# Down-projections of two feed-forward networks by Strassen's seven products, and the order of the second mixer's tiles

## The chip, the cores and the metric

One core of one Trainium2 chip runs the whole program. The metric is the device time of one execution in microseconds. Three runs of the kernel before took 2653.42, 2655.38 and 2654.62 us; the median is 2654.62 us. The profiled execution, from which all rows come, is a run of its own.

## The reference

Two transformer-like blocks run one after the other on a sequence of 1024 positions of width 1024, in float32. Each has a mixer and a feed-forward network (FFN). Cut to what the change touches, with x of shape 1024 x 1024:

```python
# first block: D_FF = 2816, second block: 4096
a, b = split(dwconv3(rms_norm(x) @ w_up), 2)     # w_up: 1024 x 5632
x = x + gate * rms_norm((gelu(a) * b) @ w_down)  # w_down: 2816 x 1024
...                                              # second mixer: four branches, gates
h = rms_norm(x) @ w_up_2                         # 1024 x 4096
x = x + rms_norm(square(relu(h)) @ w_down_2)     # w_down_2: 4096 x 1024
```

The two products by `w_down` and `w_down_2` are the down-projections. Their inner dimension is 22 and 32 tiles of 128 hidden units.

## The kernel before, in words

A float32 matrix is kept as a pair of narrower ones, a high part (fp32r, made by a cast on ScalarE) and a low part (what is left, made by a subtraction on VectorE): `split`, L345 to L347. One product is then three matmuls, high by high, high by low and low by high. All large matmuls are of one size: a stationary block of 128 x 128 and a moving one of 128 x 512.

The up-projections and the gates of the second mixer already use Strassen's scheme (`strassen`, L205 to L258). It takes a pair of weight blocks as a 2 x 2 matrix of blocks and the activations as another, and makes seven products (84 matmuls) where eight would do. The sums of activation quarters that the products need are made once per stage by `act_sums` (L318 and the splits behind it), the sums of weights by `_pair` (L144).

The down-projections don't. `ffn` (L615 to L640) computes hidden units and stores each tile of 128 units, 512 KB, to DRAM through ScalarE's DMA queue (L619, tensors `hd`). `Down` (L565 to L612) then takes the units in groups of k-tiles, 2, 2, 2, 4, 4, 4, 4 in the first FFN and 2, 2 and seven times 4 in the second. For a k-tile, `prep` loads the weight tile and the hidden tile (512 KB each, issued by SyncE, L583) and splits both. For a group, `rows` (L485 to L500) goes through the eight row tiles of the output, and for each through the k-tiles of the group with six matmuls each; `rows_sum` adds the two PSUM halves to the output tile in SBUF (copies by ScalarE in the first group, L507, VectorE additions afterwards, L509). `prep` of the next group stands between the row tiles.

In the second mixer, before the gates, a short convolution (`sc_y`, L1411 to L1418) and `act_sums` are written one after the other, in the order three steps of the convolution, a half of the sums, one step, the other half, the rest (L1780 to L1787). The results of the branches go to DRAM (`br`, L1733) and come back (`st`) for the branch projections.

Each engine executes its instructions in order. That order is set when the kernel is built, by a scheduler that works from the program as it is written and from the buffers of the tile pools. A tile pool with n buffers makes the writer of tile i wait until all readers of tile i - n have finished.

Of the kernel before, what the change touches and what calls it, by code (L numbers as in the profile page):

```python
# [55 lines left out]
def drive(*streams):  # L56
# [3 lines left out]
    while live:  # L60
# [50 lines left out]
class Weights:  # L111
# [72 lines left out]
    def next(self, n=1, room=None, slow=False):  # L184
# [4 lines left out]
        if self.begun < len(self.units):  # L189
# [123 lines left out]
def act_sums(k, act, place, tmp):  # L313
# [8 lines left out]
    for j in range(2):  # L322
# [239 lines left out]
class Down:  # L562
# [25 lines left out]
    def first(self):  # L588
        for _ in range(self.sizes[0]):
            self.prep(0)  # L590

    def run(self, pool, bnd):
        k = self.k
        Y = [pool.tile([P, T], F32, name=f"y{m}") for m in range(8)]
        n = len(self.sizes)
        for G in range(n):
# [7 lines left out]
            for tt in range(8):  # L604
                ps = (row_halves if last or tt % 2 == 0 else row_pair)(k)
                rows(k, parts, lhs, tt, ps)
                rows_sum(k, ps, Y[tt], G == 0)
                if last:
                    bnd.row(Y, tt)
                elif tt % 2 == 1 and len(self.got) < self.sizes[G + 1]:  # L610
                    self.prep(G + 1)


def ffn(k, w, act, n, head, tail, sizes, bnd):
# [3 lines left out]
    hd = [k.dp.tile([P, T], F32, name=f"hd{n}_{i}") for i in range(n)]  # L618
    out = lambda i, t: k.nc.scalar.dma_start(out=hd[i], in_=t)  # L619
    with ExitStack() as whole:  # L620
# [3 lines left out]
        dn = Down(k, w, hd, sizes, place)  # L624
        with ExitStack() as c:
# [15 lines left out]


def ffn1(k, w, act, bnd):
# [27 lines left out]
    def head(spare, sums, out):  # L671
        pg, pv = halves(k, w, act)
        next(sums)
# [4 lines left out]
        next(sums)  # L678
# [1446 lines left out]
```

## Time and profile before

| | |
|---|---|
| median of three runs | 2654.62 us |
| profiled execution | 2655.48 us |
| its span, first to last instruction | 2653.7 us |
| TensorE matmuls busy | 2565.7 us, 11972 matmuls |
| VectorE busy | 1793.3 us |
| ScalarE busy | 1080.3 us |
| DMA | 267.07 MB |

Outside the span lie 1.8 us. Busy shares are means over stages with different limits, so the rows below are taken by stage. Between 560 and 900 us the first FFN's up-projection runs, from 928 to about 1160 its down-projection, up to about 1465 and beyond the second mixer, from 1468 its gates, from 2298 the second down-projection. In a timeline a bracket behind an instruction holds the idle time of its engine just before it and what ended it.

### The profile page before, as it was taken

To read this page: it belongs to the slowest core of one execution; us is meant where nothing else is said; L and a number is where in the kernel's file an instruction comes from. 1 tells how busy PE (TensorE), PEld (TensorE's weight loads), DVE (VectorE), ACT (ScalarE), POOL (GpSimd) and SP (SyncE) were. 2 spreads that over 40 slices of the span, in tenths; PEclk is the share of its full clock that TensorE was granted. 3 is DMA by queue.
4 is the path that set the end of the run, shared out by engine and by line. 5 is a ranking of instruction groups with operands and counts; after the bars stand their busy time and mean duration, and the time that the engine had idled before them with its cause. 6 is when DMAs were issued, how large, how long until landed. Compare 5 with 4: busy or idle time off the path is not lost.

```text
span 2653.7 us, 30737 instructions
## 1 busy us (share of the span) xinstructions
PE 2565.7 (97%) x11972; PEld 2090.8 (79%) x11972; DVE 1793.3 (68%) x2882; ACT 1080.3 (41%) x1604; POOL 0.2 (0%) x4
## 2 busy tenths in 40 slices
PE   5999999899999999999999899999999999999998
PEld 4886777778888788878877688888878888888886
DVE  8778757888888863385779765665667545454435
ACT  6444746544444431174343433233365444521211
POOL 0000000000000000000000000000000000000000
PEclk9999999899999999999999999999999999999999
DMA  7315424122222352131012222222342333642312
GB/s 256 97 51 171 136 64 151 54 87 80 84 75 96 130 187 80 48 132 48 32 40 73 78 80 77 98 80 73 103 150 88 103 119 103 204 136 97 107 53 103
DMA packets 85653, 267.07 MB, mean 101 GB/s; under 512 B 12545, under 2 KB 22145, under 8 KB 85506
## 3 DMA queue, kind: packets, MB, share of 16 engines
q1 hardware_dynamic: 76002, 230.49, 26.4%
q10 hardware_dynamic: 9504, 34.61, 3.3%
q8 instruction: 94, 1.54, 0.2%
q14 instruction: 53, 0.43, 0.1%
HBM read 210.53 MB, written 54.53 MB: 100 GB/s over the span
## 4 chain that ended last, share of the span: by engine, by line
PE 83%; DVE 10%; ACT 3%; DMA 2%; issue 1%; SPq 0%; ACTq 0%; DVEq 0%
PE ps_p L233 23%; PE ps_q L233 12%; PE ps_row L496 5%; PE ps_row L498 5%; PE ps_row L500 5%; PE ps_rows L496 4%; PE ps_rows L498 4%; PE ps_rows L500 4%; PE ps_z L217 3%; PE ps_z L213 3%; PE ps_z L215 3%; PE ps_bo L217 1%; PE ps_bo L215 1%; PE ps_bo L213 1%; PE ps_o L1177 1%
## 5 line engine op out<-in xcount | busy, mean ns | idle before, releaser
L346 ACT CAST whi<-wraw 128x1024 fp32r<-128x1024 f32 x232 | 243.2, 1051 | 516.1 <-DVE wraw L144 156.8
L347 DVE TENSOR_TENSOR wlo<-wraw,whi 128x1024 fp32r<-128x1024 f32 x232 | 283.0, 1222 | 174.9 <-ACT whi L346 174.6
L233 PE MATMUL ps_p<-s,whi 128*128 128x512 f32 x792 | 247.0, 393 | 0.2 <-DVE s L347 0.2
L509 DVE TENSOR_TENSOR y<-y,ps_row 128x512 f32<-128x512 f32 x160 | 103.3, 682 | 136.9 <-PE ps_row L500 136.9
L233 PEld LDWEIGHTS ps_p<-s,whi 128*128 128x128 f32 x792 | 148.9, 188 | 33.6 <-DVE s L347 0.6
L233 PE MATMUL ps_p<-s,wlo 128*128 128x512 f32 x396 | 155.3, 392 | 0.0
L509 DVE TENSOR_TENSOR y<-y,ps_rows 128x512 f32<-128x512 f32 x112 | 71.8, 682 | 109.9 <-PE ps_rows L500 109.9
L233 PE MATMUL ps_q<-s,whi 128*128 128x512 f32 x408 | 125.9, 389 | 0.3 <-ACT y L245 0.3
L375 ACT ACTIVATE junk<-y 128x1024 bf16<-128x1024 f32 x56 | 59.1, 1056 | 154.8 <-DVE y L481 69.8
L144 DVE TENSOR_TENSOR wraw<-wraw,wraw 128x512 f32<-128x512 f32 x150 | 103.7, 691 | 11.5 <-DMA wraw<-in_W 7.1
L240 DVE TENSOR_TENSOR sg<-sg,ps_p 128x512 f32<-128x512 f32 x79 | 54.1, 685 | 69.2 <-PE ps_p L233 63.6
L240 DVE TENSOR_TENSOR y<-y,ps_p 128x512 f32<-128x512 f32 x85 | 58.1, 684 | 49.3 <-PE ps_p L233 48.6
L240 DVE TENSOR_TENSOR y<-y,ps_q 128x512 f32<-128x512 f32 x83 | 56.8, 684 | 48.9 <-PE ps_q L233 48.7
L346 ACT CAST s<-s 128x1024 fp32r<-128x1024 f32 x30 | 31.6, 1053 | 143.1 <-PE ps_rows L498 124.2
L233 PEld LDWEIGHTS ps_q<-s,whi 128*128 128x128 f32 x408 | 76.5, 188 | 16.6 <-ACT y L245 0.7
L233 PEld LDWEIGHTS ps_p<-s,wlo 128*128 128x128 f32 x396 | 74.5, 188 | 16.6
L346 ACT CAST dnh<-s 128x1024 fp32r<-128x1024 f32 x24 | 25.2, 1049 | 134.9 <-PE ps_rows L498 120.5
L233 PE MATMUL ps_q<-s,wlo 128*128 128x512 f32 x204 | 79.4, 389 | 0.0
L496 PE MATMUL ps_row<-whi,s 128*128 128x512 f32 x240 | 75.3, 393 | 3.2 <-ACT y L507 1.8
L500 PE MATMUL ps_row<-whi,s 128*128 128x512 f32 x240 | 75.1, 393 | 0.0
L498 PE MATMUL ps_row<-wlo,s 128*128 128x512 f32 x240 | 74.7, 391 | 0.0
L498 PE MATMUL ps_rows<-dnl,dnh 128*128 128x512 f32 x192 | 59.1, 389 | 0.0
(734 smaller groups left out, 6762.9 us busy)
## 6 DMA issues: line engine op xcount, KB each, us to landing
wraw<-in_W SPq DMA_DIRECT2D x216, 512.0 KB, 3.8
s<-hd SPq DMA_DIRECT2D x54, 512.0 KB, 4.7
scr<-in_wa SPq DMA_DIRECT2D x32, 512.0 KB, 4.3
hd<-y ACTq DMA_DIRECT2D x28, 512.0 KB, 4.7
xr<-y SPq DMA_DIRECT2D x24, 512.0 KB, 2.8
hd<-cg ACTq DMA_DIRECT2D x22, 512.0 KB, 2.6
wa<-in_wa SPq DMA_DIRECT2D x16, 512.0 KB, 4.8
xl<-xr SPq DMA_DIRECT2D x16, 512.0 KB, 4.8
```

Of the source, the lines that this page charges most:

```text
L144: less = lambda o, x, y: self.k.nc.vector.tensor_tensor(out=o, in0=x, in1=y, op=ALU.subtract)
L213: nc.tensor.matmul(ps(h), lhsT=wh, rhs=xh[:, cut(h)], start=a, stop=False)
L215: nc.tensor.matmul(ps(h), lhsT=wh, rhs=xl[:, cut(h)], start=False, stop=False)
L217: nc.tensor.matmul(ps(h), lhsT=wl, rhs=xh[:, cut(h)], start=False, stop=z)
L233: mm = lambda x, y, start=False, stop=False: nc.tensor.matmul(ps, lhsT=x, rhs=y, start=start, stop=stop, skip_group_check=True)
L240: add = lambda o, x, y: V.tensor_tensor(out=o, in0=x, in1=y, op=ALU.add)
L346: k.nc.scalar.copy(hi, x)
L347: k.nc.vector.tensor_tensor(out=lo, in0=x, in1=rr(hi), op=ALU.subtract)
L496: nc.tensor.matmul(ps[c], lhsT=xh, rhs=wh[:, S2H[c]], start=a, stop=False)
L498: nc.tensor.matmul(ps[c], lhsT=xh, rhs=wl[:, S2H[c]], start=False, stop=False)
L500: nc.tensor.matmul(ps[c], lhsT=xl, rhs=wh[:, S2H[c]], start=False, stop=z)
L509: k.V.tensor_tensor(out=o, in0=o, in1=ps[c], op=ALU.add)
```

## The change

The down-projections take most of their hidden tiles four at a time. Such a batch is a 2 x 2 matrix of blocks on the side of the hidden units (two k-tiles by 512 positions each) and on the side of the weights (two k-tiles by 512 outputs). It goes through seven products, in the order p1, p6, p2, p7, p5, p4, p3. A product of one batch is a step: 24 matmuls, into four PSUM banks. The batches of a group go through a product one after the other, and its banks are summed over them; then the banks are added to the output tiles or to a partial sum `u`. `DOWN1` has one group of four batches, then plain groups of 2 and 4 k-tiles; `DOWN2` has groups of four and three batches, then a plain group of 4. The plain groups keep the old code.

`load` issues the DMAs of a step three steps ahead: a hidden quarter or a weight quarter is 512 KB, in runs of 2 KB. `prep` makes the factors of a step two steps ahead: sums (L645), then splits (L360, L361). The split hidden factor has three buffers (`s4`/`s5`, `s6`/`s7`, `s8`/`s9` by step number modulo 3), the split weight factor three, the raw hidden tiles four in rotation.

In the second mixer `act_sums` hands back control four times per half, short convolution and sums are interleaved by `drive` with costs, and the temporaries of the sums are in a pool of their own.

```diff
-    def run(self, pool, bnd):
-        k = self.k
-        Y = [pool.tile([P, T], F32, name=f"y{m}") for m in range(8)]
+    ORDER = ("p1", "p6", "p2", "p7", "p5", "p4", "p3")
+    AHEAD = 2
...
+        self.steps = [(g, p, b) for g, nb in enumerate(groups) for p in self.ORDER for b in range(nb)]
...
+    def raw(self):
+        self.raws += 1
+        if self.raws % 2:
+            return self.place(10 + self.raws // 2 % 2, [P, 2, H], F32)
+        return self.k.wp.tile([P, 2, H], F32, tag="raw", bufs=2, name="hraw")
...
+        def hidden(r, c, t=None):
+            t = t or self.raw()
+            src = self.hb[at].rearrange("(a k) p c -> k p a c", k=2)[c]
+            nc.sync.dma_start(out=t, in_=src[:, :, S2H[r]])
+            return t
...
+        if p == "p1":
+            self.s2[b] = hidden(0, 0, self.place(b, [P, 2, H], F32))
+            weights(0, 0)
+            weights(0, 1)
+        elif p == "p6":
+            self.x[g, p, b] = [hidden(1, 0), hidden(1, 1)]
+            weights(1, 1)
+        elif p == "p2":
+            self.x[g, p, b] = [hidden(0, 1)]
+            weights(1, 0)
+        else:
+            self.x[g, p, b] = [hidden(r, c) for r, c in dict(p7=((0, 0), (1, 0)), p5=((1, 0), (1, 1)), p4=((1, 1),), p3=((0, 1),))[p]]
...
+        elif p == "p6":
+            tt(x[0], x[0], x[1], Ad)
+            a = self.s2[b]
+            tt(a, x[0], a, Su)
+            tt(w11, w12, w11, Su)
+            w = self.raw()
+            tt(w, w22, w11, Su)
...
+        r = i % 3
+        lhs = [self.place(4 + 2 * r + c, [P, 2, H], F32R) for c in range(2)]
+        split(k, *lhs, a)
+        rhs = [k.wp.tile([P, 2, H], F32R, tag=t, bufs=3, name=t) for t in ("whi", "wlo")]
+        split(k, *rhs, w)
...
+            for a in range(2):
+                for t in range(4):
...
+                    mm(lhs[0], rhs[0], start=fresh and a == 0)
+                    mm(lhs[0], rhs[1])
+                    mm(lhs[1], rhs[0], stop=a == 1)
+            self.load()
+            if i + self.AHEAD < n:
+                self.prep(i + self.AHEAD)
...
+                if p == "p6" and last and not one:
+                    for t in range(4):
+                        for y in (Y[4 + t][:, h], Y[4 + t][:, l], Y[t][:, h]):
+                            V.tensor_tensor(out=y, in0=y, in1=u[t], op=ALU.add)
...
+DOWN1 = (4,), (2, 4), (True, False)
+DOWN2 = (4, 3), (4,), (True,)
...
-    ffn(k, w, act, 22, head, tail, [2, 2, 2, 4, 4, 4, 4], bnd)
+    ffn(k, w, act, 22, head, tail, DOWN1, bnd)
...
-    ffn(k, w, act, 32, head, tail, [2, 2] + [4] * 7, bnd)
+    ffn(k, w, act, 32, head, tail, DOWN2, bnd)
...
-        sums = act_sums(k, act, place, lambda name: k.t4.tile([P, 2, H], F32, tag="sg", name=name))
-        for _ in range(3):
-            next(sc)
-        next(sums)
-        next(sc)
-        next(sums)
-        finish(sums)
-        keep(3, finish(sc))
+        sums = act_sums(k, act, place, lambda name: k.wx.tile([P, 2, H], F32, tag="xs", bufs=4, name=name))
...
+        drive((short(), 43.6), (sums, 29.2))
```

Three places show how the instructions stand now. The first is VectorE at the start of the first FFN's down-projection. Before, in the second group of k-tiles, there are additions of PSUM halves (`ps_row`, `ps_rows`) to output tiles, and now and then a split (`dnl`):

```order
L509 TENSOR_TENSOR y4_7187<-y4_7187,ps_row_7425 128x512 [waits PE_49]
L509 TENSOR_TENSOR y4_7187<-y4_7187,ps_row_7426 128x512 [waits PE_49]
L509 TENSOR_TENSOR y5_7188<-y5_7188,ps_rows_7441 128x512 [waits PE_49]
L509 TENSOR_TENSOR y5_7188<-y5_7188,ps_rows_7441 128x512
L509 TENSOR_TENSOR y6_7189<-y6_7189,ps_row_7456 128x512 [waits DMAHW5_49,PE_49]
L509 TENSOR_TENSOR y6_7189<-y6_7189,ps_row_7457 128x512 [waits PE_49]
L347 TENSOR_TENSOR dnl_7525<-s0_7526,dnh_7524 128x1024 [waits DMAHW4_49,PE_49,Activation_49]
L509 TENSOR_TENSOR y7_7190<-y7_7190,ps_rows_7472 128x512 [waits PE_49]
```

Now, in the steps of p6 (steps 4 to 7; `s0` to `s3` are hidden quarters kept for the four batches, `s10`, `s11` and `hraw` raw tiles, `dw` weight quarters):

```order
L361 TENSOR_TENSOR s5_7399<-s2_7123,s4_7398 128x1024 [waits PE_49,Activation_49]
L361 TENSOR_TENSOR wlo_7403<-s11_7396,whi_7402 128x1024 [waits Activation_49]
L645 TENSOR_TENSOR s10_7387<-s10_7387,hraw_7389 128x1024 [waits DMAHW6_49,DMAHW2_49]
L645 TENSOR_TENSOR dw_7115<-dw_7259,dw_7115 128x1024
L645 TENSOR_TENSOR s3_7217<-s10_7387,s3_7217 128x1024 [waits DVE_49]
L361 TENSOR_TENSOR s9_7476<-hraw_7430,s8_7475 128x1024 [waits DMAHW3_49,PE_49,Activation_49]
L645 TENSOR_TENSOR s10_7437<-dw_7391,dw_7219 128x1024 [waits DVE_49]
L361 TENSOR_TENSOR s7_7440<-s3_7217,s6_7439 128x1024 [waits Activation_49]
L361 TENSOR_TENSOR s5_7512<-hraw_7471,s4_7511 128x1024 [waits DMAHW5_49,PE_49,Activation_49]
L361 TENSOR_TENSOR wlo_7444<-s10_7437,whi_7443 128x1024 [waits Activation_49]
```

Row by row these are the lower half for step 6, its weights, three sums for step 7, the hidden lower half for step 8, a sum for step 7, the lower half for step 7, the hidden lower half for step 9 (`s5` from `s4_7511`) and the weights of step 7 (`wlo_7444`). ScalarE's casts of the same factors, now:

```order
L360 CAST s4_7398<-s2_7123 128x1024 [waits DVE_49,Activation_49]
L360 CAST whi_7402<-s11_7396 128x1024 [waits DVE_49,Activation_49]
L360 CAST s8_7475<-hraw_7430 128x1024 [waits DMAHW3_49,PE_49,Activation_49]
L360 CAST s6_7439<-s3_7217 128x1024 [waits DVE_49]
L360 CAST s4_7511<-hraw_7471 128x1024 [waits DMAHW5_49,PE_49,Activation_49]
L360 CAST whi_7443<-s10_7437 128x1024 [waits DVE_49]
L360 CAST whi_7479<-dw_7432 128x1024 [waits DMAHW7_49]
```

The cast for step 9 (`s4_7511`) stands ahead of the cast of step 7's weights (`whi_7443`); it overwrites what step 6 reads.

The second place is VectorE in the same phase of the second FFN, now (its first group; before, these rows were additions as above):

```order
L645 TENSOR_TENSOR hraw_17111<-hraw_17111,s11_17113 128x1024 [waits DMAHW7_49,DMAHW1_49]
L645 TENSOR_TENSOR dw_16902<-dw_17072,dw_16902 128x1024
L645 TENSOR_TENSOR s2_16904<-hraw_17111,s2_16904 128x1024 [waits DVE_49]
L645 TENSOR_TENSOR s11_17171<-dw_17115,dw_16906 128x1024 [waits DMAHW2_49]
L645 TENSOR_TENSOR s10_17162<-s10_17162,hraw_17164 128x1024 [waits DMAHW6_49,DMAHW2_49]
L361 TENSOR_TENSOR s5_17174<-s2_16904,s4_17173 128x1024 [waits PE_49,Activation_49]
L361 TENSOR_TENSOR wlo_17178<-s11_17171,whi_17177 128x1024 [waits Activation_49]
L645 TENSOR_TENSOR s3_16992<-s10_17162,s3_16992 128x1024 [waits DVE_49]
```

The sum into `s10_17162` reads `hraw_17164`, which takes the buffer of `hraw_17111`. That one is read last by the sum into `s2_16904`, two rows ahead, so the load of `hraw_17164` is issued only when that row is done.

The third place is TensorE at the first pair of the gates in the second mixer. Before, the second half of the first product bank (`a12`) stands behind two other pieces of work:

```order
L233 MATMUL ps_p_11255<-a11h_8464,wlo_11159 128x512
L233 MATMUL ps_p_11257<-a22h_8475,whi_11260 128x512 [waits DVE_49,Activation_49]
L233 MATMUL ps_p_11257<-a22l_8477,whi_11260 128x512
L233 MATMUL ps_p_11256<-s4_11124,whi_11169 128x512 [waits Activation_49]
L233 MATMUL ps_p_11256<-s6_11126,whi_11169 128x512 [waits DVE_49]
L233 MATMUL ps_p_11256<-s4_11124,wlo_11170 128x512
L233 MATMUL ps_p_11256<-s4_11124,whi_11169 128x512
L233 MATMUL ps_p_11256<-s6_11126,whi_11169 128x512
L233 MATMUL ps_p_11256<-s4_11124,wlo_11170 128x512
L233 MATMUL ps_p_11258<-s8_11128,whi_11260 128x512
L233 MATMUL ps_p_11258<-s10_11130,whi_11260 128x512
L233 MATMUL ps_p_11255<-a12h_8467,whi_11158 128x512 [waits Activation_49]
```

Now it stands directly behind the first half (`a11`):

```order
L244 MATMUL ps_p_11243<-a11h_8452,whi_11158 128x512
L244 MATMUL ps_p_11243<-a11l_8454,whi_11158 128x512
L244 MATMUL ps_p_11243<-a11h_8452,wlo_11159 128x512
L244 MATMUL ps_p_11243<-a12h_8455,whi_11158 128x512 [waits Activation_49]
L244 MATMUL ps_p_11243<-a12l_8457,whi_11158 128x512
L244 MATMUL ps_p_11243<-a12h_8455,wlo_11159 128x512
```

What the `a12` matmuls wait for is a copy by ScalarE (`sg`). Before, ScalarE has there:

```order
L346 CAST whi_11260<-wraw104_11154 128x1024 [waits DVE_49,PE_49]
L346 CAST s4_11124<-xa22_11134 128x1024 [waits DVE_49]
L1733 DMA br3_1_9009<-sc_y_11149 128x1024 [waits DMAHW1_49,DVE_49]
L346 CAST s4h_11239<-xa11_11139 128x1024 [waits DVE_49]
L346 CAST s9_11129<-xa22_11224 128x1024 [waits DMAHW7_49,DVE_49]
L346 CAST bt_11388<-st_11390 128x1024 [waits DMAHW2_49]
L242 COPY sg_11253<-ps_p_11255 128x512 [waits DVE_49,PE_49]
```

Now:

```order
L360 CAST s4_10996<-xa22_11006 128x1024 [waits DVE_49]
L360 CAST bt_11370<-st_11372 128x1024 [waits DMAHW7_49]
L360 CAST s4h_11227<-xa11_11011 128x1024 [waits DVE_49,PE_49]
L360 CAST s9_11001<-xa22_11079 128x1024 [waits DMAHW5_49,DVE_49]
L360 CAST s1_10993<-xa21_11077 128x1024 [waits DVE_49]
L360 CAST whi_11169<-wraw105_11156 128x1024 [waits DVE_49]
L1914 DMA br3_1_8997<-sc_y_11149 128x1024 [waits DVE_49]
L360 CAST s5_10997<-xa22_11079 128x1024 [waits DVE_49]
L253 COPY sg_11241<-ps_p_11243 128x512 [waits PE_49]
```

Ahead of the copy stand now the cast of `bt`, which reads a branch that has been to DRAM and back, and the casts of `s4h`, `s1`, `whi_11169` and `s5`, whose sums VectorE makes first.

## Rows read from the trace of the kernel before

**Rows 1.** The page: span; busy time, share, count by engine.
```profile
span 2653.7 us, 30737 instructions
PE 2565.7 (97%) x11972; PEld 2090.8 (79%) x11972; DVE 1793.3 (68%) x2882; ACT 1080.3 (41%) x1604; POOL 0.2 (0%) x4
```

**Rows 2.** The chain that ended last, by engine; one piece: start, us, what.
```profile
PE 83%; DVE 10%; ACT 3%; DMA 2%; issue 1%; SPq 0%; ACTq 0%; DVEq 0%
...
591.21 19.04 PE ps_p L233 x84
```

**Rows 3.** Windows: length, busy PE PEld DVE ACT POOL, granted clock, DMA share, GB/s.
```profile
912.00:930.00 18.00, 16.19 (x68) 12.71 (x67) 15.23 (x14) 10.45 (x15) 0.00 (x0) 0.98 0.68 231
960.00:1100.00 140.00, 140.00 (x620) 115.91 (x619) 75.45 (x94) 32.46 (x32) 0.00 (x0) 1.00 0.35 113
1460.00:1480.00 20.00, 12.93 (x48) 9.51 (x47) 18.36 (x17) 9.13 (x10) 0.00 (x0) 0.80 0.27 92
1480.00:1500.00 20.00, 19.27 (x79) 15.23 (x78) 18.83 (x22) 10.59 (x13) 0.00 (x0) 0.95 0.22 69
2292.00:2310.00 18.00, 17.50 (x78) 14.17 (x77) 8.46 (x8) 13.84 (x20) 0.00 (x0) 1.00 0.88 307
2310.00:2600.00 290.00, 290.00 (x1281) 240.23 (x1280) 133.30 (x165) 58.83 (x61) 0.00 (x0) 1.00 0.30 99
```

**Rows 4.** Groups by line and shape: busy us, mean ns | idle before, releaser.
```profile
L347 DVE TENSOR_TENSOR wlo<-wraw,whi 128x1024 fp32r<-128x1024 f32 x232 | 283.0, 1222 | 174.9 <-ACT whi L346 174.6
L346 ACT CAST whi<-wraw 128x1024 fp32r<-128x1024 f32 x232 | 243.2, 1051 | 516.1 <-DVE wraw L144 156.8 <-PE ps_p L233 134.0 <-PE ps_q L233 87.4
L509 DVE TENSOR_TENSOR y<-y,ps_row 128x512 f32<-128x512 f32 x160 | 103.3, 682 | 136.9 <-PE ps_row L500 136.9
```

**Rows 5.** VectorE's chain of five sums without a pause (start, us, what).
```profile
1471.08 5.68 DVE xa L318 x5
```

**Rows 6.** DMA issues: count, KB each, median us to landing.
```profile
s<-hd SPq DMA_DIRECT2D x54, 512.0 KB, 4.7
U<-uj_d SPq DMA_DIRECT2D x3, 512.0 KB, 4.1
uy<-U SPq DMA_DIRECT2D x3, 512.0 KB, 5.4
```

**Rows 7.** Landing of the hidden tiles, and of `uy`.
```profile
DMA to landing us min/median/max: 2.6/4.4/7.0
...
DMA to landing us min/median/max: 2.7/5.4/6.6
```

**Rows 8.** TensorE at the two down-projections and the gates: start, us, instruction [idle].
```profile
927.69 0.99 PE L496 MATMUL ps_row<-whi,s 128*128 128x512 f32 x2 [1.81 <-ACT y L507]
...
1467.50 0.39 PE L233 MATMUL ps_p<-a11h,wlo 128*128 128x512 f32 x1
...
1470.02 0.47 PE L233 MATMUL ps_p<-a22h,whi 128*128 128x512 f32 x1 [2.13 <-DVE sc_y L1418]
1471.13 0.50 PE L233 MATMUL ps_p<-s,whi 128*128 128x512 f32 x1 [0.19 <-DVE s L347]
1478.62 0.79 PE L233 MATMUL ps_p<-a12h,whi 128*128 128x512 f32 x1 [4.75 <-ACT sg L242]
1495.54 0.50 PE L233 MATMUL ps_p<-a12h,whi 128*128 128x512 f32 x1 [0.73 <-ACT sg L242]
...
2297.84 0.73 PE L496 MATMUL ps_rows<-whi,s 128*128 128x512 f32 x2 [0.50 <-DVE y L240]
```

**Rows 9.** VectorE and ScalarE around the gates' first pair (start, us, instruction).
```profile
1464.11 1.23 DVE L347 TENSOR_TENSOR bt<-st,bt 128x1024 fp32r<-128x1024 f32 x1 [1.64 <-ACT bt L346]
1481.21 1.22 DVE L347 TENSOR_TENSOR wlo<-wraw,whi 128x1024 fp32r<-128x1024 f32 x1
...
1477.98 0.59 ACT L242 COPY sg<-ps_p 128x512 f32<-128x512 f32 x1 [0.33 <-DVE s4l L347]
```

**Rows 10.** The branch's way to DRAM and back, in the chain.
```profile
1454.05 3.56 DMA br<-sc_y
1457.66 5.34 DMA st<-br
```

More of the change, by code (lines that the diff above doesn't have):

```diff
@@ L72, in drive, with skip @@
             s[2] += c
+def skip(gen, n):
+    for _ in range(n):
+        next(gen)
 def finish(gen):
@@ new lines, in prep @@
+    def prep(self, i):
+        k, V = self.k, self.k.nc.vector
+        Ad, Su = ALU.add, ALU.subtract
+        tt = lambda o, x, y, op: V.tensor_tensor(out=o, in0=x, in1=y, op=op)
+        g, p, b = self.steps[i]
+        x = self.x.pop((g, p, b), None)
+        w11, w12, w21, w22 = (self.wt.get((r, c, b)) for r in range(2) for c in range(2))
+        if p == "p1":
+            a, w = self.s2[b], w11
+        elif p == "p6":
[5 more added lines that the diff above has]
+            tt(w, w22, w11, Su)
+        elif p == "p2":
+            a, w = x[0], w21
+        elif p == "p7":
+            a, w = x[0], w12
+            tt(a, a, x[1], Su)
+            tt(w, w22, w, Su)
+        elif p == "p5":
+            a, w = x[0], w11
+            tt(a, a, x[1], Ad)
+        elif p == "p4":
+            a, w = x[0], w21
+            tt(w, w, w22, Su)
+            tt(w, w, w11, Ad)
+        else:
+            a, w = x[0], w22
+            tt(a, a, self.s2[b], Su)
+        r = i % 3
[3 more added lines that the diff above has]
+        split(k, *rhs, w)
+        self.ready[i] = lhs, rhs
@@ L610, in run, with ffn @@
                 elif tt % 2 == 1 and len(self.got) < self.sizes[G + 1]:
-                    self.prep(G + 1)
-def ffn(k, w, act, n, head, tail, sizes, bnd):
+                    self.plain(G + 1)
+DOWN1 = (4,), (2, 4), (True, False)
+DOWN2 = (4, 3), (4,), (True,)
+def ffn(k, w, act, n, head, tail, down, bnd):
     tc = k.tc
-    hd = [k.dp.tile([P, T], F32, name=f"hd{n}_{i}") for i in range(n)]
-    out = lambda i, t: k.nc.scalar.dma_start(out=hd[i], in_=t)
     with ExitStack() as whole:
@@ L628, in ffn @@
             sums = act_sums(k, act, place, lambda name: cp.tile([P, 2, H], F32, tag="c4", bufs=9, name=name))
-            with ExitStack() as cq:
-                k.pmm = tp("pmmh", cq, bufs=2, space=PSUM)
-                head(tile_, sums, out)
+            with ExitStack() as ch:
+                k.pmm = tp("pmmh", ch, bufs=2, space=PSUM)
+                head(tile_, sums, dn.out)
             finish(sums)
-            with ExitStack() as cq:
-                k.pmm = tp("pmms", cq, space=PSUM)
-                tail(tile_, out, dn.first)
+            k.pmm = tp("pmms", cq, space=PSUM)
+            tail(tile_, dn.out, dn.first)
         with ExitStack() as c:
             pool = tp("fd", c)
+            dn.Y = [pool.tile([P, T], F32, name=f"y{m}") for m in range(8)]
+            dn.products(pool)
+            cq.close()
             k.pmm = tp("pmmd", c, bufs=2, space=PSUM)
             k.bd = bound_tiles(pool)
-            dn.run(pool, bnd)
+            dn.rest(bnd)
 def ffn1(k, w, act, bnd):
@@ L705, in head @@
         first = halves(k, w, act)
-        next(sums)
+        skip(sums, 4)
         for f in range(4):
@@ L1869, in ffn_order @@
             out += [("pair",) + u(f), ("and",) + u(f + 1)]
-    return out + [("row", down, f) for f in range(n)]
+    return out + [("row" if f >= paired else "more" if f else "other", down, f) for f in range(n)]
 BRANCHES = [3, 1, 2, 0]
@@ L1894, in weight_units @@
 def weight_units():
-    return [("pair" if kind == "pair" else "one", n) for n, (kind, _, _) in enumerate(weight_order()) if kind != "and"]
+    kinds = dict(pair="pair", other="other")
+    return [(kinds.get(kind, "one"), n) for n, (kind, _, _) in enumerate(weight_order()) if kind not in ("and", "more")]
 def pack_weights(d):
```

125 lines of the change are left out of this document (103 added, 22 removed).

## The prediction

> **What bounds the kernel now.** I read the page first: the reader is to see TensorE busy for 97% of the span with VectorE at 68% and ScalarE at 41% [rows 1]. Then the chain of waits: TensorE carries 83% of the time, VectorE 10%, DMA 2% [rows 2]. Then the windows by stage: in the first down-projection TensorE is busy for all 140 of 140 us, VectorE for 75 (54%) and ScalarE for 32, and in the second for 290 of 290 [rows 3]. So in these stages a matmul less is its time less, until something else is late. A piece of the chain gives the price of one: 84 matmuls in 19.04 us, 0.2267 us each [rows 2] (the 0.39 us of a single one are its passage, not its pace). One place is different: from 1460 to 1480 us TensorE works 12.93 of 20 us, beside a VectorE busy for 18.36, and the granted clock is 0.80 [rows 3]; there the timeline shows stalls of 2.13, 0.19, 4.75 and, at 1495.54, 0.73 us [rows 8], 7.80 together. VectorE bounds that place.
>
> **The change part by part.** *Matmuls.* Four k-tiles took 4 x 8 x 6 = 192 matmuls, and take 7 x 24 = 168. There are 4 + 7 = 11 batches, so 264 matmuls go: 264 x 0.2267 = **-59.85 us**. The 77 steps left are 24 x 0.2267 = 5.44 us each, 419 us, where the same k-tiles took 478.8.
>
> *VectorE's work for the products.* A batch needs 14 lower halves and 10 sums. A lower half alone takes 1.22 us [rows 4]; five in a row take 5.68 us, 1.14 each [rows 5]. So a batch costs 27.4 to 29.3 us against 38.1 of TensorE. The additions of banks are 28 of 0.68 us [rows 4] a group, fewer than those they replace. On average VectorE keeps up and all this is hidden. Step by step it does not: a p6 step has four sums and two lower halves, 6 x 1.22 = 7.3 us against 5.44. All other products need 2.4 to 4.9. ScalarE has two casts of 1.05 [rows 4], 2.1 us a step.
>
> *The first group's p6.* The order shows more than the average. ScalarE casts step 9's hidden factor ahead of step 7's weights, VectorE does the same with the lower halves, and that buffer is free only when step 6's matmuls have ended. From there step 7 waits for a cast (1.05), a lower half (1.22) and its own (1.22): 3.5 us, 3.7 with the signals between them. Nothing hides it. Walking down VectorE's rows from the tail's last convolution (each starts at the latest of: the row ahead, its buffer, its transfer), I find steps 5 and 6 another 2.3 us late, since each costs 1.8 us over the pace and the lead is under two steps. After such gaps the granted clock was 0.98 and 0.80 in the windows with stalls of 1.81 us and of 4.75 us [rows 3, 8]; I add 1.5. **+7.5**, bounds 3.7 and 18.
>
> *The second FFN's first group.* Its order has no such swap, but the sum into s10 waits for a load whose buffer is freed two rows ahead. A hidden tile lands 4.4 us after issue in the median, 2.6 to 7.0 at the ends [rows 7]; one row of 1.22 us stands between, so VectorE idles some 3.2, plus issue 0.4, in a phase that is already behind: 3.6, and 1.0 for the clock. **+4.6**, bounds 0 (the lead covers it) and 18.
>
> *The second group of the second FFN.* Twelve additions of 128 x 512 in SBUF stand at the end of p6 in front of the next factors: 12 x 0.68 = 8.2 us. They have as cover three p2 and p7 steps; I take **+1.5**, bounds 0 and 8.
>
> *Transitions.* A group of plain k-tiles begins today 1.81 us after the tail in the first FFN and 0.50 in the second [rows 8]. The first product needs factors of the same size from the same queues: 0, bounds -2 and +4. The plain rest is unchanged.
>
> *Mixer.* Now VectorE makes all sums of both halves ahead of the second weights' lower half (39 rows behind the last multiplication of the convolution in its order, before 30), and ScalarE's copy stands behind casts that need these sums. The first half of the bank ends at 1467.5 + 0.4 [rows 8]. Before, the copy ran at 1477.98 [rows 9], but two other pieces of matmul work stood ahead of what waits for it. By VectorE's rows at 1.14 us each from the same start, and with bt behind a trip of 3.56 + 5.34 us through DRAM [rows 10], I put the copy at 1481.5, so TensorE idles about 14 us in one piece; the second weights' lower half comes nine rows later, some of them half as long, near 1488.4 instead of 1481.21 [rows 9]. The pair's 84th matmul then ends about 6 us later: **+6**. Bounds: -7.8 if the new order removes all stalls, +10 if the branch's trip takes another 4 us, as a landing varies by 7.0 - 2.6 [rows 7].
>
> *DMA.* A batch moves 14 blocks of 0.524 MB: 7.34 MB, 80.7 MB in 419 us, 193 GB/s; in p1 and p6 three blocks a step are 289 GB/s. Today the stages move 99 to 113 GB/s, but 307 GB/s stand in the 18 us from 2292 at a DMA share of 0.88 with TensorE busy for 17.50 [rows 3]. The new pieces are 2 KB long at a 4 KB pitch, which no row of before has. Nearest are transfers in short pieces, U from uj_d in 4.1 us and uy from U in 5.4, against 4.7 for whole hidden tiles [rows 6]. I take 4.7, with three steps (16.3 us) of lead: 0.
>
> The Trainium skill ("DMA: Bandwidth & Descriptors", section "Latency and other measured facts") speaks against this: copies whose rows lie at a power-of-two pitch in HBM get slower as the pitch grows, from 207 GB/s at 512 KiB to 164 at 2 MiB. Rows here are 4 KB apart, far below; no row of this trace shows a large pitch. By 164 GB/s the products would take 492 us, 73 more than 419, an estimate from that page, and with the mixer's 6 the change would lose 19 us.
>
> Sum: -59.85 + 7.5 + 4.6 + 1.5 + 6 = -40.3. Against the profiled execution (2653.7 + 1.8 = 2655.5) that gives 2615.2; this execution stands 0.9 us above the median of the runs, so I forecast **2615 us**, rounded.
>
> **The rivals.** *B, all is covered.* Steps 5 and 6 and the second FFN's p6 have enough lead, and the mixer stays as it is: -59.85 + 3.7 = -56.2, **2599 us**. For it: VectorE needs 29.3 of 38.1 us a batch. Against: p6 comes second, right behind the cheap p1, with a lead of two steps.
>
> *C, the landing chain.* Loads wait for buffers in every p6 step: 2.3 us of work, a landing of 7.0 [rows 7] and 0.3 make 9.6 us, 4.2 over the pace. Four steps less a lead of 5 us lose 12, three steps 8: 32 for the three groups. With 3.7 for the swap, 6 for the mixer and 5.5 for the clock: -59.85 + 47.2 = -12.6, **2643 us**. For it: the demand of 289 GB/s is just below the 307 seen. Against: the median landing is 4.4.
>
> *D, the other side: the half rows are too slow.* If one transfer takes the 6.6 us that uy needs at the worst [rows 7] and two run at a time, that is 159 GB/s: 80.7 MB take 508 us, 89 more than 419. -59.85 + 89 + 6 = +35, **2690 us**. It decides as soon as the products get less than 176 GB/s (80.7 MB in 419 + 40 us). Against: 307 GB/s in a stretch that holds hidden tiles and weights.
>
> **How the numbers follow.** Forecast (between 2604 and 2630) 0.62, B 0.17, C 0.13, D 0.06, other 0.02. The range is **2597 to 2643**: it holds the forecast, B and the lower part of C, and leaves out D and half of C. A measurement of this kernel tells no change from about 0.2%, 5.3 us. Forecast, B and nearly all of C are faster by more than that: 0.90. Same: the upper end of C, 0.03. Slower: D and a little of C, 0.07.
>
> **What would show it.** In the changed profile: 264 matmuls fewer and steps of 5.44 us in long runs; a gap of 3 to 4 us at TensorE in front of step 7 of the first FFN, with VectorE's lower half as its end; a gap of a few us in p6 of the second FFN behind a DMA; in the mixer one gap of 10 to 15 us behind the copy to sg and a granted clock below 0.9 around it; hidden quarters landing in 4 to 6 us. Wrong would be: gaps in every p6 step that end with a DMA (C), a DMA share near 1 through whole products (D), no gap over 2 us in the mixer, or 90% of the saving kept (B).
>
> The Trainium skill ("TensorE: Matmul & The Clock Gate", section "Part 1: The HAM clock gate") says that an idle TensorE is clocked at 1.2 GHz until activity releases it. The granted clock of 0.80 beside the 4.75 us gap [rows 3, 8] agrees; by that rule the mixer's long gap would cost some time on top of itself, which lies within the bounds above.

## The result and the profile after

The changed kernel takes 2590.09 us in the median of four runs (2588.34 to 2598.13), the kernel before, run beside it, 2654.02. The ratio is 0.9769, with a 95% interval from 0.9752 to 0.9786. The change gains 63.9 us; the forecast was 2615 us, a gain of 40, with a range from 2597 to 2643. The direction was right, the time lies 7 us outside the range.

The profiled execution of the changed kernel is the slowest of its four, 2598.13 us. The page's first lines, to be read beside [rows 1]:

```profile
span 2595.8 us, 30381 instructions
PE 2501.1 (96%) x11708; PEld 2044.8 (79%) x11708; DVE 1925.6 (74%) x2950; ACT 1144.8 (44%) x1666; POOL 0.2 (0%) x4
```

There are 264 matmuls fewer, as counted, yet TensorE is busy for 64.6 us less where 264 x 0.2267 are 59.9. I cut both spans at the same matmuls and compare the pieces:

| piece | before | after | difference |
|---|---|---|---|
| start to first matmul of the first down-projection | 914.73 | 918.28 | +3.6 |
| from there to the second mixer's first matmul | 252.40 | 232.73 | -19.7 |
| to the first matmul of the gates | 297.88 | 297.83 | 0.0 |
| first pair of the gates, to the second pair | 26.91 | 31.55 | +4.6 |
| rest of the gates and output projection, to the second FFN | 482.49 | 472.50 | **-10.0** |
| second FFN's up-projection | 320.05 | 321.34 | +1.3 |
| second down-projection, to the end | 359.24 | 321.57 | -37.7 |

The sum is -57.9, the difference of the spans. The first row lies ahead of anything that the change touches. There TensorE waits 2.07 us for a lower half of VectorE where the kernel before waits 0.96, and the matmuls behind that wait run at the lower clock level (granted clock 0.62 from 60 to 64 us). By 64 us the changed kernel is 3.8 us late, and it stays so (TensorE, after first):

```profile
58.16 0.74 PE L226 MATMUL ps_z<-actl,whi 128*128 128x512 f32 x2 [2.07 <-DVE actl L361]
...
60.77 1.05 PE L224 MATMUL ps_z<-acth,whi 128*128 128x512 f32 x2
```
```profile
56.01 0.74 PE L215 MATMUL ps_z<-actl,whi 128*128 128x512 f32 x2 [0.96 <-DVE actl L347]
```

The row that hardly any part of the prediction spoke of is the one of -10.0: the gates, whose matmuls are the same in number and operands. About 0.8 of it is the stall of 0.73 us at 1495.54 [rows 8], which is gone; the rest is pace. TensorE is busy for all of 100 us in both kernels at a clock of 1.00, and does 433 matmuls before, 443 and 442 after (before first; columns as in [rows 3]):

```profile
1600.00:1700.00 100.00, 100.00 (x433) 81.21 (x433) 67.40 (x82) 31.81 (x38) 0.00 (x0) 1.00 0.29 95
1700.00:1800.00 100.00, 100.00 (x433) 81.19 (x432) 63.01 (x78) 31.76 (x38) 0.00 (x0) 1.00 0.23 74
```
```profile
1600.00:1700.00 100.00, 100.00 (x443) 82.81 (x442) 69.24 (x85) 32.54 (x40) 0.00 (x0) 1.00 0.28 95
1700.00:1800.00 100.00, 100.00 (x442) 82.79 (x442) 64.34 (x81) 32.36 (x39) 0.00 (x0) 1.00 0.25 79
```

Nothing waits there, so neither the chain nor a list of waits can show it; the count per window does.

In the products TensorE stands still three times, twice in the first FFN's p6 and once in the second's. In the gates there is one gap (timeline of TensorE after: start, us, instruction, idle before it and what ended it; they answer to [rows 8]):

```profile
947.05 0.50 PE L708 MATMUL ps_p<-wlo,s 128*128 128x512 f32 x1 [0.85 <-DVE wlo L361]
960.71 2.05 PE L708 MATMUL ps_p<-whi,s 128*128 128x512 f32 x4 [2.90 <-ACT whi L360]
...
1451.34 0.39 PE L244 MATMUL ps_p<-a11h,wlo 128*128 128x512 f32 x1
1464.03 0.79 PE L244 MATMUL ps_p<-a12h,whi 128*128 128x512 f32 x1 [12.30 <-ACT sg L253]
...
1469.31 0.42 PE L244 MATMUL ps_p<-a22h,whi 128*128 128x512 f32 x1
...
2313.44 0.50 PE L708 MATMUL ps_p<-wlo,s 128*128 128x512 f32 x1 [0.52 <-DVE wlo L361]
```

Behind the gap of 12.30 us twelve matmuls take 1464.03 to 1469.31, 0.44 us each, about twice the usual: the clock is at its lower level (granted clock 0.50 from 1464 to 1469 us). The Trainium skill ("TensorE: Matmul & The Clock Gate", section "Part 1: The HAM clock gate") has an idle TensorE clocked at 1.2 GHz; these rows agree. This costs 2.5 us, but the kernel before has such a stretch there too: its eight matmuls from 1478.62 to 1482.18 take 0.44 us each (granted clock 0.50). So the 4.6 in the table come from the idle time, 12.30 us against 2.13 + 0.19 + 4.75 = 7.07 [rows 8].

In the second FFN's p6 only the wait of 0.52 us is left, and what ends it is VectorE's own lower half, not a load. VectorE works without a pause, and the loads come fast (windows after: p1 of the first FFN, then p6 of the second):

```profile
918.00:940.00 22.00, 22.00 (x98) 18.22 (x98) 22.00 (x20) 8.50 (x9) 0.00 (x0) 1.00 0.99 367
...
2296.00:2318.00 22.00, 21.48 (x95) 17.48 (x94) 22.00 (x21) 9.28 (x11) 0.00 (x0) 1.00 0.86 293
```

### The profile page after: what moved, and what is told of

It is laid out like the page before. It is cut to its first block, busy times and chain, and to the rows that moved or that the text cites. A ratio compares the mean times of both kernels' runs of the same rounds, so it can differ in the third digit from the quotient of the medians.

```text
span 2595.8 us, 30381 instructions
## 1 busy us (share of the span) xinstructions
PE 2501.1 (96%) x11708; PEld 2044.8 (79%) x11708; DVE 1925.6 (74%) x2950; ACT 1144.8 (44%) x1666; POOL 0.2 (0%) x4
## 4 chain that ended last, share of the span: by engine, by line
PE 81%; DVE 14%; ACT 3%; issue 2%; DMA 1%; SPq 0%; ACTq 0%; DVEq 0%
PE ps_p L244 24%; PE ps_q L244 12%; PE ps_q L708 7%; PE ps_p L708 6%; PE ps_z L226 3%; PE ps_z L228 3%; PE ps_z L224 3%; PE ps_row L510 2%; PE ps_row L512 2%; PE ps_row L514 2%; DVE xa L329 1%; DVE wlo L361 1%; PE ps_o L1358 1%; PE ps_bo L224 1%; PE ps_bo L228 1%
## 5 line engine op out<-in xcount | busy, mean ns | idle before, releaser
L360 ACT CAST whi<-wraw 128x1024 fp32r<-128x1024 f32 x211 | 221.7, 1051 | 498.0 <-DVE wraw L149 155.5
L361 DVE TENSOR_TENSOR wlo<-wraw,whi 128x1024 fp32r<-128x1024 f32 x211 | 257.9, 1223 | 165.5 <-ACT whi L360 165.3
L708 PE MATMUL ps_q<-whi,s 128*128 128x512 f32 x656 | 204.5, 391 | 0.0
L708 PE MATMUL ps_p<-whi,s 128*128 128x512 f32 x576 | 180.1, 391 | 2.9 <-ACT whi L360 2.9
L708 PEld LDWEIGHTS ps_q<-whi,s 128*128 128x128 f32 x656 | 123.6, 189 | 26.1 <-DVE s L361 0.4
L360 ACT CAST s<-s 128x1024 fp32r<-128x1024 f32 x63 | 66.4, 1053 | 163.3 <-PE ps_q L708 43.0
L708 PEld LDWEIGHTS ps_p<-whi,s 128*128 128x128 f32 x576 | 108.5, 189 | 25.8 <-ACT whi L360 3.3
L708 PE MATMUL ps_q<-wlo,s 128*128 128x512 f32 x328 | 127.6, 389 | 0.0
L708 PE MATMUL ps_p<-wlo,s 128*128 128x512 f32 x288 | 112.4, 390 | 1.4 <-DVE wlo L361 1.4
L361 DVE TENSOR_TENSOR s<-s,s 128x1024 fp32r<-128x1024 f32 x63 | 77.1, 1223 | 22.4 <-ACT s L360 22.3
L361 DVE TENSOR_TENSOR wlo<-dw,whi 128x1024 fp32r<-128x1024 f32 x66 | 80.5, 1221 | 9.2 <-ACT whi L360 9.1
```

What stands on the lines that cost most here:

```text
L360: k.nc.scalar.copy(hi, x)
L361: k.nc.vector.tensor_tensor(out=lo, in0=x, in1=rr(hi), op=ALU.subtract)
L708: mm = lambda x, y, start=False, stop=False: nc.tensor.matmul(banks[t], lhsT=x[:, a, o], rhs=y[:, a], start=start, stop=stop, skip_group_c ...
```

## The experiments

### What sets the pace in the gates

The change widens a small tile of the second mixer from `[P, 32]` to `[P, 128]`. All tiles of that mixer lie behind it in SBUF. In the built programs each tile's start address can be read: before, the mixer's tiles start at 192 modulo 512 bytes, and weights and activations at 64; after, all start at 64. Two theories: the placement sets the pace, or the new order and the moved temporaries do. The first experiment makes that one edit to the kernel before:

```diff
-    k.mp = Cut(tp("m2s").tile([P, 32], F32, name="small"))
+    k.mp = Cut(tp("m2s").tile([P, 128], F32, name="small"))
```

> The kernel before with one edit: the second mixer's tile of small values is 512 bytes wide per partition, not 128. Every tile of that mixer that is allocated behind it then starts at 64 modulo 512 bytes, as the tiles of all other stages do, where it started at 192. Nothing is reordered. Theory P (placement sets the pace of the matmuls in the gates): the pace between 1500 and 1850 us goes from 433 to about 442 matmuls in 100 us, and the time falls by 8 to 10 us, to about 2645; the stalls of 2.13 and 4.75 us at the gates' start stay. Rival Q (the new order or the moved temporaries of the sums set it, by what VectorE does meanwhile): no change, within 2 us, 433 in 100 us.

2644.46 us beside 2654.44, ratio 0.9961 (0.9948 to 0.9973), and the pace went up:

```profile
1600.00:1700.00 100.00, 100.00 (x443) 82.81 (x442) 67.64 (x83) 31.82 (x38) 0.00 (x0) 1.00 0.28 95
```

Theory P holds: one tile's width is worth 10 us in the medians. In the profile, the table's row of the gates and the output projection falls from 482.49 to 473.25, by 9.2. Within a product, 18 matmuls with `s` took 1535.26 to 1539.46 before, 0.2333 us each, and here 1534.81 to 1538.89, 0.2267 (before first):

```profile
1535.26 0.63 PE L233 MATMUL ps_p<-s,whi 128*128 128x512 f32 x2
...
1539.46 0.63 PE L233 MATMUL ps_p<-s,whi 128*128 128x512 f32 x2
```
```profile
1534.81 0.62 PE L233 MATMUL ps_p<-s,whi 128*128 128x512 f32 x2
...
1538.89 0.62 PE L233 MATMUL ps_p<-s,whi 128*128 128x512 f32 x2
```

Which tiles, and what about the place? Next, only the pool of the split sums was moved, with the split weight quarters behind it, in the kernel before:

```diff
         sp, k.wx = tp("m2s4", cs), tp("m2wx", cs)
+        sp.tile([P, 96], F32, tag="pad", name="pad")
```

> The kernel before with 384 bytes of padding ahead of the pool of the split sums (s0 to s11) alone: these and the split weight quarters behind them start at 64 modulo 512 bytes, the sums, gates and branch tiles (sg, bt, st, ys) stay at 192. Theory S (a matmul is slowed by where its own operand lies): the gates' products with s and s4 go to 0.2267 us each, the branch projections, which read bt, stay at 0.232; 1600 to 1700 us shows 440 or more matmuls, and the kernel gains 4 to 7 of the 10 us that aligning all of the mixer's tiles gave. Rival T (tiles that VectorE, ScalarE and the DMAs work on, t4's, disturb TensorE where they lie apart from its operands): 433 to 435 matmuls, gain under 2 us.

2645.97 us, ratio 0.9973 (0.9962 to 0.9984). The gates reach 440 matmuls in 100 us, while the output projection behind them, one of whose operands (`x`, then `bt`) still starts at 192, stays slow: 172 in 40 us, 178 with all tiles aligned (the aligned run first):

```profile
1860.00:1900.00 40.00, 40.00 (x178) 32.81 (x177) 24.61 (x28) 19.47 (x27) 0.00 (x0) 1.00 0.24 80
```
```profile
1600.00:1700.00 100.00, 100.00 (x440) 82.25 (x440) 67.83 (x84) 32.10 (x39) 0.00 (x0) 1.00 0.28 96
...
1860.00:1900.00 40.00, 40.00 (x172) 32.08 (x172) 22.71 (x26) 17.44 (x25) 0.00 (x0) 1.00 0.24 79
```

So a matmul is slowed by its own operands' places (theory S), not by those of the tiles that other engines work on. Then everything was shifted, in the changed kernel by 128 bytes:

```diff
     cp, k.sm = tp("const"), tp("small")
+    cp.tile([P, 32], F32, name="pad")
```

> The changed kernel with 128 bytes of padding at the start of SBUF: the tiles of all stages, weights and activations too, start at 192 modulo 512 bytes, where they start at 64. Theory A (the place itself counts): all stages with large matmuls take 0.231 us a matmul, 2 percent more; about 40 us slower than the changed kernel, 2630. Rival R (tiles only have to lie alike, whatever the place): pace and time as the changed kernel, 2590, within 4 us.

2588.21 us, ratio to the kernel before 0.9759 (0.9742 to 0.9776), the changed kernel's time; 443 matmuls. Rival R: the tiles have to lie alike, the place itself is free. By 448 bytes, on the products with the old mixer order, the old temporaries and the wide small tile:

> The products alone with the old mixer, with its small tile widened and 448 bytes of padding at the start of SBUF, so that the tiles of all stages start at a multiple of 512 bytes. From the earlier run of the products alone (2598) and the 10 us that the aligned mixer gave, the same with all tiles at 64 would take 2588. Theory A0 (64 is itself a place that costs, 0 is better): a matmul comes below 0.2267 us, at best 0.2133, the time of 512 columns at 2.4 GHz, so up to 140 us faster. Rival: 64 and 0 are alike, 2588 within 4 us.

2587.13 us, ratio 0.9755 (0.9741 to 0.9770), again 443: the hoped-for gain at 0 isn't there. Last, how far is apart? The small tile of the kernel before at 256 and at 192 bytes (`[P, 64]`, `[P, 48]`):

> The kernel before with the small tile at 256 bytes: the second mixer's tiles start at 320 modulo 512 bytes, 256 from all others, where they were 128 from them (192) and ran slow, and 0 from them (64) and ran fast. If the pattern repeats every 256 bytes: 442 matmuls in 100 us and about 2644. If every 512: slow, 433 or fewer, 2654 or more.

> The kernel before with the small tile at 192 bytes: the second mixer's tiles start at 256 modulo 512 bytes, 64 away (modulo 256) from weights and activations, where 128 away ran slow and 0 away fast. Theory half (any difference modulo 256 costs as much): 433 matmuls in 100 us, 2653. Rival (a difference of 128 alone, or less cost for a smaller one): between 436 and 443, 2644 to 2650.

The first took 2645.22 us, ratio 0.9969 (0.9959 to 0.9979), with 443 matmuls in 100 us; the second 2652.96, ratio 0.9991 (0.9980 to 1.0002), with 435 (first and second):

```profile
1600.00:1700.00 100.00, 100.00 (x443) 82.81 (x442) 67.27 (x82) 32.87 (x40) 0.00 (x0) 1.00 0.27 95
```
```profile
1600.00:1700.00 100.00, 100.00 (x435) 81.12 (x434) 67.43 (x82) 31.67 (x38) 0.00 (x0) 1.00 0.27 95
```

In the second, 18 matmuls with `s` took 1533.82 to 1538.02, again 0.2333 us each:

```profile
1533.82 0.63 PE L233 MATMUL ps_p<-s,whi 128*128 128x512 f32 x2
...
1538.02 0.63 PE L233 MATMUL ps_p<-s,whi 128*128 128x512 f32 x2
```

Distances of 0 and 256 are fast, 64 and 128 slow, by about the same (435 and 433 matmuls): theory half. All of this is seen with fp32r matmuls of 128 x 512 alone. Why the chip does so no run shows.

### The products alone, and the mixer's order

The changed kernel with the second mixer as it was, narrow small tile and temporaries included:

```diff
-    k.mp = Cut(tp("m2s").tile([P, 128], F32, name="small"))
+    k.mp = Cut(tp("m2s").tile([P, 32], F32, name="small"))
...
-        sums = act_sums(k, act, place, lambda name: k.wx.tile([P, 2, H], F32, tag="xs", bufs=4, name=name))
...
-        drive((short(), 43.6), (sums, 29.2))
+        sums = act_sums(k, act, place, lambda name: k.t4.tile([P, 2, H], F32, tag="sg", name=name))
+        for _ in range(3):
+            next(sc)
+        skip(sums, 4)
+        next(sc)
+        skip(sums, 4)
+        finish(sums)
+        keep(3, finish(sc))
```

> The changed kernel with the second mixer as it was (order, temporaries, narrow small tile), so the products of the down-projections alone. From the two profiles the down-projections lost 19.7 and 37.7 us: theory, 57 us faster than before, about 2597, with the gates at 433 matmuls in 100 us and stalls of about 7 us at their start. Rival (the forecast's sizes of the waits in p6 hold in other executions): 46 us, about 2608.

2598.14 us, ratio 0.9789 (0.9775 to 0.9803): 56.3 us gained beside 2654.44, with 434 matmuls in 100 us. So the products alone give 56, not the 46 that the forecast's terms make without the mixer.

The edit of the order alone, with the moved temporaries and the wide tile kept:

> The changed kernel with the convolution and the sums of the second mixer in the old order; temporaries and small tile stay as changed. Theory: the one gap of 12.3 us at the gates' start goes back to stalls of about 7 us, the gates keep 442 matmuls in 100 us, and the kernel is 4 to 5 us faster than the changed one, about 2585. Rival: the old order brings the slow pace back, 433 in 100 us, and the kernel is about 4 us slower than the changed one, 2594. Second rival: the temporaries alone had made the stalls, and nothing changes.

2585.57 us, ratio 0.9746 (0.9728 to 0.9764). The gates keep 443 matmuls, so the order has no part in the pace. In the old order the gap is shorter, though one piece of 8.62 us and not the stalls of before:

```profile
1452.33 0.79 PE L244 MATMUL ps_p<-a12h,whi 128*128 128x512 f32 x1 [8.62 <-ACT sg L253]
```

The medians differ by 4.5 us and their intervals overlap; the gap in the profile, 3.7 us less, is the firmer number, and the first pair of the gates takes 27.36 us in place of 31.55, 4.2 less. The new order costs about that, as the forecast's sign had it.

### The first FFN's p6

Four buffers for the split hidden factor, in the changed kernel:

```diff
-        r = i % 3
+        r = i % 4
...
-            return self.place(10 + self.raws // 2 % 2, [P, 2, H], F32)
+            return self.place(12 + self.raws // 2 % 2, [P, 2, H], F32)
```

> The changed kernel with four buffers for the split hidden factor of a step in place of three; the order of the products stays. Theory: the wait of 2.90 us in front of step 7 of the first FFN comes from step 9's factor, which overwrites what step 6 reads; with four buffers it goes, with the lower clock behind it: 3 to 5 us faster than the changed kernel, about 2586. Rival: VectorE is late in p6 by its own work (six operations of 1.22 against 5.44 us), then the wait only moves, under 1.5 us gained.

2585.56 us, ratio 0.9740 (0.9722 to 0.9758), 4.5 below the changed kernel. The wait of 2.90 us is gone, VectorE's lateness stays:

```profile
947.16 0.50 PE L708 MATMUL ps_p<-wlo,s 128*128 128x512 f32 x1 [0.74 <-DVE wlo L361]
953.97 0.50 PE L708 MATMUL ps_p<-wlo,s 128*128 128x512 f32 x1 [0.60 <-DVE wlo L361]
```

So the wait did come from step 9's factor in the buffer that step 6 reads. The gain in time is less firm than the gap: the two intervals overlap at 0.9752 to 0.9758.

Loads written a step later, `for _ in range(self.AHEAD)` in `first`:

> The changed kernel with the loads of a step written two steps ahead of its matmuls in place of three. Theory L (the third step of lead hides the landings of 3.7 to 6.6 us in p6): VectorE then waits for transfers in p6, 2 to 4 us a step where its own work is already over the pace, so 10 to 25 us slower than the changed kernel, 2600 to 2615. Rival B (SyncE issues a load as soon as its buffer is free, wherever it is written, and the buffers set that): within 4 us of 2590.

2590.62 us, ratio 0.9757 (0.9741 to 0.9773): no change in the time, which rival B has right. The profile doesn't leave p6 as it was, though. VectorE now waits 1.68 us for a load there, as theory L says, and the waits of TensorE, 0.85 and 2.90 us in the changed kernel, are 2.10 and 1.22 here (VectorE, then TensorE, of this run):

```profile
943.53 1.23 DVE L645 TENSOR_TENSOR s<-s,hraw 128x1024 f32<-128x1024 f32 x1 [1.68 <-DMA hraw<-hb]
```
```profile
948.16 0.50 PE L708 MATMUL ps_p<-whi,s 128*128 128x512 f32 x1 [2.10 <-ACT s L360]
957.66 0.50 PE L708 MATMUL ps_p<-whi,s 128*128 128x512 f32 x1 [1.22 <-ACT s L360]
```

The order of VectorE's sums and ScalarE's casts in p6 changed with the edit too, and in sum nothing is lost: the first FFN's stage takes 232.54 us, in the changed kernel 232.73. So what the lead of three steps (16.3 us) is worth as cover is not shown.

### Both gains together, and GpSimd

Old order and four buffers:

> The changed kernel with both edits that gained: the old order in the second mixer and four buffers for the split hidden factor. Theory (the two gains are in different stages and add): 4.5 and 4.5 us below the changed kernel's 2590, about 2581; the gaps in the profile are 8.6 us at the gates' start and under 1 us each in p6. Rival (a gain of one is a clock loss that the other has too): 2585.

2583.38 us, ratio 0.9725 (0.9711 to 0.9740), which is below the changed kernel's interval and the best but one. Between 2581 and 2585 the time doesn't decide. The profile, cut as in the table, shows both gains side by side: the first FFN's stage takes 227.58 us (232.73 in the changed kernel, 228.53 with four buffers alone), the first pair of the gates 27.39 (31.55, and 27.36 with the old order alone). With six sums on GpSimd besides:

```diff
-            tt(t, rr(act.q[n][0][j]), rr(act.q[n][1][j]), Ad)
+            (V or k.nc.vector).tensor_tensor(out=t, in0=rr(act.q[n][0][j]), in1=rr(act.q[n][1][j]), op=Ad)
...
+        sums = act_sums(k, act, place, lambda name: k.wx.tile([P, 2, H], F32, tag="xs", bufs=4, name=name), k.nc.gpsimd)
```

> As the run with both gains, and six of the sums in the second mixer's act_sums (high plus low part of a quarter) go from VectorE to the idle GpSimd. Theory (VectorE's row of sums is what the copy to sg waits for): 6 x 1.14 = 7 us less of VectorE ahead of it, the gap of 8.6 us falls to 2 to 5 and the kernel is 3 to 6 us below the run with both gains, about 2577. Rival (GpSimd is slower at these sums, or slows VectorE beside it): the copy waits for GpSimd instead, 0 to 8 us slower, up to 2589.

2580.99 us, ratio 0.9719 (0.9704 to 0.9733), the fastest here, but only 2.4 us below the last, with overlapping intervals, and the stages show no gain: the first pair of the gates takes 28.16 us in place of 27.39, and the profiled execution is ahead by 3.8 us at the first down-projection already, before any sum on GpSimd. The gap was halved and a second one of the same size appeared, since a sum takes GpSimd 2.37 us or more where VectorE needs 1.22, and a cast that TensorE waits for, `s4h`, comes late (GpSimd, then TensorE, of this run):

```profile
1445.70 2.37 POOL L336 TENSOR_TENSOR xa<-a11h,a11l 128x1024 f32<-128x1024 f32 x1 [4.63 <-DVE xa L329]
```
```profile
1446.83 0.72 PE L244 MATMUL ps_p<-a22h,whi 128*128 128x512 f32 x1 [4.20 <-ACT s4h L360]
1453.04 0.80 PE L244 MATMUL ps_p<-a12h,whi 128*128 128x512 f32 x1 [4.20 <-ACT sg L253]
```

VectorE is slowed beside it, as the rival says: a lower half that starts while GpSimd works on a sum takes 3.43 us in place of 1.22 and ends 1.1 us after that sum (GpSimd, then VectorE):

```profile
1437.74 3.32 POOL L336 TENSOR_TENSOR xa<-a22h,a22l 128x1024 f32<-128x1024 f32 x1 [6.50 <-DVE s L361]
```
```profile
1438.71 3.43 DVE L361 TENSOR_TENSOR wlo<-wraw,whi 128x1024 fp32r<-128x1024 f32 x1
```

## Why the prediction was wrong

Its largest term and its account of what bounds the kernel held. Six smaller terms erred, all to the same side; the one that took the time out of the range is the pace in the gates.

- **Matmuls, -59.85.** Right: 264 fewer, at 0.2267 us.
- **The pace in the gates, not in the sum.** This is the main failure. The widened small tile stood in the diff and got no price; I took every 128 x 512 matmul at the pace of one piece of the chain [rows 2], which lies in the first FFN. The same view holds the gates, 433 matmuls in 100 us where 441 would be that pace. Measured: -10.0 in the gates and behind; that edit alone gave 10 us in the medians and 9.2 in this stage, and the rest is the stall of 0.73 us that went. With the 10 us in the sum the forecast would have been 2605, still 15 too high; without them the kernel would have taken about 2600, inside the range.
- **The first group's p6, +7.5.** The swap was as forecast (3.7 foreseen, 2.90 measured, at step 7), though what ends it is ScalarE's cast of step 7's weights and not VectorE's lower half, the sign that I had named. Steps 5 and 6 lost 0.85 where I had 2.3. The stage took 2.1 us more than its 96 matmuls fewer would make it (21.8 - 19.7).
- **Transitions, 0.** The wait of 1.81 us [rows 8] and the low clock behind it went away. I had misread its place: the group begins at 914.73 without a wait, and the 1.81 us stand in front of its fifth row tile, where TensorE waits for ScalarE to copy a bank. Product p1 sums four steps in its banks, so the first copy is due after 21.8 us. That low clock cost about 2.0 us before: the 18 matmuls from 927.69 to 933.77 took 6.1 us where 18 x 0.2267 are 4.1 (before; each row is the first of three of a kind). So the products' own loss is 2.1 + 3.8 = 5.9, of 7.5, and -3.8 belongs to the transition.

```profile
929.64 1.05 PE L496 MATMUL ps_row<-whi,s 128*128 128x512 f32 x2
932.20 0.82 PE L496 MATMUL ps_rows<-whi,s 128*128 128x512 f32 x2
933.77 0.61 PE L496 MATMUL ps_rows<-whi,s 128*128 128x512 f32 x2
```

- **The second FFN's first group, +4.6.** Failed: no wait for a load; the one wait in p6 is 0.52 us, for VectorE's own lower half, and the wait of 0.50 us of before [rows 8] went. The step that failed is "a load whose buffer is freed two rows ahead". I had given `hraw_17164` the buffer of `hraw_17111`, in the section on the change too. The trace shows SyncE issuing that load at 2297.52, right behind the lower half `wlo_17127` at 2296.27, so its buffer is that of `hraw_17120`, free six rows ahead of the sum; in the built program these two start at one address. The sum into `s10` starts at 2303.08 without a wait (VectorE, and SyncE's issue, after):

```profile
2296.27 1.23 DVE L361 TENSOR_TENSOR wlo<-hraw,whi 128x1024 fp32r<-128x1024 f32 x1
2297.40 1.23 DVE L645 TENSOR_TENSOR dw<-dw 128x1024 f32<-128x1024 f32 x1
...
2301.94 1.23 DVE L645 TENSOR_TENSOR s<-dw 128x1024 f32<-128x1024 f32 x1
2303.08 1.23 DVE L645 TENSOR_TENSOR s<-s,hraw 128x1024 f32<-128x1024 f32 x1
```
```profile
2297.52 0.37 SPq L617 DMA_DIRECT2D hraw<-hb  x1
```

- **The second group, +1.5.** TensorE has no gap there: 0. The lead covers the twelve additions.
- **The mixer, +6.** The gap is 12.30 us where 14 was forecast, and the pair 4.6 us later, of which 0.8 comes back in the next pair. The copy comes right behind the cast of a split sum that VectorE makes late, as the order had it (ScalarE after):

```profile
1462.44 1.04 ACT L360 CAST s<-xa 128x1024 fp32r<-128x1024 f32 x1 [3.49 <-DVE xa L329]
1463.39 0.58 ACT L253 COPY sg<-ps_p 128x512 f32<-128x512 f32 x1
```

- **DMA, 0.** Right in what it cost. The hidden quarters land in 3.7 to 4.3 us, but the weight quarters in 6.6 where I had taken 4.7 for all (median, last column, answering to [rows 6]); why they are slower is not shown. In p1 the first FFN moved 367 GB/s with TensorE busy throughout, and no gap of TensorE in the products ends with a load. That ends rivals C and D. The DMA share of 0.99 in that window is the sign that I had named for D, and TensorE lost nothing: the sign was badly chosen. The Trainium skill's rule on row pitches ("DMA: Bandwidth & Descriptors", section "Latency and other measured facts") was rightly kept out of the sum: hidden quarters, whose rows are 4 KB apart, landed no later than the 4.7 us of whole tiles [rows 6].

```profile
s<-hb SPq DMA_DIRECT2D x59, 512.0 KB, 4.3
hraw<-hb SPq DMA_DIRECT2D x51, 512.0 KB, 3.7
dw<-in_W SPq DMA_DIRECT2D x44, 512.0 KB, 6.6
```

With the measured terms the sum is -59.85 + 5.9 - 3.8 + 0.4 + 4.6 - 10.0 = -62.8, where 0.4 is what the second down-projection lost beside its 168 matmuls (38.1 - 37.7). The medians say -63.9. The profiled execution's own -57.9 has +3.6 and +1.3 besides, from stretches ahead of the products: the first begins with the wait of 2.07 us shown above, the second holds waits of 0.67 and 0.26 us that the kernel before doesn't have. Why these came isn't known. Rival B named the right idea for the second FFN, but with 2599 it too lacked the gates' 10 us.

## What to carry to other kernels

A change that resizes any tile moves every tile behind it: compare start addresses, and count matmuls per window in stages that the change leaves alone, since a slower pace has no wait and no low clock to show. When a stall is forecast from a buffer, write down which tile held that buffer last by counting the rotation tile by tile; one miscounted turn made a stall of 3.6 us out of nothing. An operation by operation walk through the order got the two largest gaps within 2 us of their sizes.

## What was not expected of the hardware

- Matmuls of 128 x 512 in fp32r ran at 0.2267 us where the two SBUF operands' start addresses were equal modulo 256 bytes, and at 0.2333 where they were 64 or 128 apart, 3% more. Where all lay alike, at 0, 64 or 192 modulo 512, the pace was the same. In the kernel before, products whose own operands lay alike, between such others, ran at 0.228 to 0.230; that is not explained.
- GpSimd took 2.37 to 3.50 us for a sum of 128 x 1024, VectorE 1.22, and a lower half of VectorE that started under such a sum took 3.43.
- Runs of one kernel lie up to 14 us apart (2640.06 to 2653.69 with the padded pool). The one case followed, the 3.6 us between the two profiles, began with a wait 1.1 us longer at 58 us and a stretch of lower clock behind it. Not every such stretch lasts: from 200 to 220 us the granted clock was 0.83 after and 1.00 before, and the 3.3 us lost there were made up by 250 us.
